# Gathering selected key and value blocks in rows of eight tokens instead of four, in a sparse-attention decoder step

## The chip, the core and the metric

The kernel runs on one core of a Trainium2 chip. Its time is device microseconds of one launch, and the median of three runs counts. The engines are named as in the profile: PE (TensorE, matmuls), PEld (its weight loads), DVE (VectorE), ACT (ScalarE), POOL (GpSimd) and SP (SyncE, which issues most transfers). A gather here is an indirect transfer that POOL issues: each partition gives a row index, and the DMA engines fetch that row from memory into that partition.

## What is computed

Two layers of a decoder run for a prompt of 1024 positions and, with the same weights, for eight samples with one new token each and 4096 past positions in paged caches. Layer 0 has three attention branches and a convolution module; layer 1 is a pooling mixer; each layer ends in a gated feed-forward network. The change touches one branch of layer 0, for the samples alone: the selected blocks.

```python
# nsa_sample, cut
o_c, p_c = compressed_attention(q, t_pos, kcmp, vcmp)      # attention over compressed tokens
idx = select_blocks(p_c, t_pos, ns)                        # 16 blocks of 64 tokens, per sample and group
key_pos = idx[..., None] * SEL_BLOCK + jnp.arange(SEL_BLOCK)
phys = page_table[bi, jnp.clip(key_pos // PAGE_SIZE, 0, n_pages - 1)]
from_pool = pool_s[li, phys, key_pos % PAGE_SIZE, :, gi]   # gather from the paged cache
...
sel = jnp.where((key_pos < past)[..., None, None], from_pool, from_new)
o_s = selected_attention(q, t_pos, idx, sel)               # softmax(q k) v over the gathered tokens
```

Each of the 8 samples has 2 key/value groups, so there are 16 lists of blocks. One block of each list is the one with the new token; the other 15 blocks of 64 tokens with 64 channels come from the cache. That is 15 x 64 x 64 x 4 bytes, or 240 KB, for each list, once for the keys and once for the values.

## The kernel before

All activations lie with channels on partitions and the 1032 columns (1024 prompt positions, then the 8 samples) along the row. The kernel runs an input projection, the compression of the prompt, prompt attention, the output projection, and two feed-forward networks with the pooling mixer between them. Each projection does its matmul in three passes of single-precision parts (`mm3`, `mm3t`). The framework orders each engine's instructions by their place in the program, a priority and its own time model, and places all waits; buffers come from pools with a fixed number of slots (the pool `u` has 16).

The samples' work is a chain of generators. `program` starts it before prompt attention, and `tick`, called after matmuls of the main stream, advances it by a clock of estimated microseconds; its steps run at a lower priority than the main stream and fill gaps in it. The chain goes: `sample_compress` (32 steps; `page_load` brings the pages of the compressed branch, half of them by POOL gathers at L571, half by SP transfers at L569), `dec_window`, `dec_select`, `dec_sel_scores`, `dec_gather_v`, `dec_values`. Prompt attention (`att_s1`, `att_s2`, `pv`) is the main stream at that time, and then `out_proj`.

The steps that the change touches:

- `dec_select` (L829) picks the blocks and turns them into row numbers `vidx`. The rows of the cache are 4 tokens long (256 numbers, 1 KB), so a block has 16 rows. Fifteen blocks are 240 rows, more than the 128 partitions, so there are two halves h: 128 rows (8 blocks) and 112 rows (7 blocks). Two matmuls (L881) spread the block numbers over the partitions.
- `dec_gather_k` (L929) makes a buffer `dw2` and four buffers `ks` of the pool `u`, two samples each, and issues 32 gathers of keys (L939): 16 lists by two halves. Nothing waits between them.
- `dec_sel_scores` (L944) starts 35 units of its clock later. For each sample and half it transposes the keys of four token places with four matmuls (L955), which read every fourth number of the rows, and ACT copies the result back over the rows it came from (the helper L105, output `ks`). Then 16 score matmuls with 512 columns and 16 with 449 (L967), the softmax into `dw2`, and eight transposes of it (L979).
- `dec_gather_v` (L985) starts when `out_proj` has set `self.after` (L1053), and issues 32 gathers of values (L996) into four buffers `vsel` of the pool `u`, which come free as prompt attention ends.
- `dec_values` (L1002) multiplies: 64 matmuls at L1027 read `vsel`.

Of the kernel before, what the change touches and what calls it, by code (L numbers as in the profile page):

```python
# [12 lines left out]
I32 = mybir.dt.int32  # L13
U32 = mybir.dt.uint32
AF = mybir.ActivationFunctionType
ALU = mybir.AluOpType
# [4 lines left out]
P = 128  # L21
D = 1024
TP = 1024
NS = 8
T = TP + NS
# [6 lines left out]
SCALE = 0.125  # L32
KY = 0.8
LAG = 100
DY = 0.6
# [5 lines left out]
class Net:  # L41
# [760 lines left out]
    def dec_prep(self):  # L802
        nc, i = self.nc, self.i
        nd = i["c_dec"].shape[1]
        dw = self.u([P, 2 * T], name="dw")
# [8 lines left out]
        cst = self.cst = dw[:, 0:nd]  # L814
        nc.sync.dma_start(cst, i["c_dec"])
        self.eb, self.own = cst[:64, 16:24], cst[:64, 358:374]
        self.pnt = d(NS, P).rearrange("p (a b) -> p a b", a=2)
# [4 lines left out]
        t = i["page_table"]  # L822
# [6 lines left out]
    def dec_select(self):  # L829
        nc, d, cst, tb = self.nc, self.d, self.cst, self.tb  # L830
        hsum = cst[:64, 0:16]
        esel, iota62, addv = cst[:16, 24:280], cst[:16, 280:342], cst[:, 342:358]
        ps = self.ps(self.to(), [64, 256])
# [44 lines left out]
        nc.vector.tensor_copy(pht, pp)  # L878
        vp = self.ps(self.to(), [P, 2, 16])
        for h in range(2):  # L880
            nc.tensor.matmul(vp[:, h], esel[:, h * P:(h + 1) * P], pht, start=True, stop=True)  # L881
        self.vidx = self.small(P, 32, I32).rearrange("p (a b) -> p a b", a=2)
        nc.vector.scalar_tensor_tensor(self.vidx, vp, 32.0, addv[:, None, :].to_broadcast([P, 2, 16]),
                                       op0=ALU.mult, op1=ALU.add)
        yield DY * 2.0
# [43 lines left out]
    def dec_gather_k(self):  # L929

        nc, i = self.nc, self.i
        self.ksel = []
        self.dw2 = self.u([P, 2 * T], name="dw2")
        for b2 in range(4):
            k = self.u([P, 2, 2, 2, 256], name="ks")
            for n in range(4):
                for h in range(2):
                    m = P - 16 * h
                    nc.gpsimd.indirect_dma_start(out=k[:m, n // 2, h, n % 2], out_offset=None, in_=i["cslc_k"],  # L939
                                                 in_offset=bass.IndirectOffsetOnAxis(  # L940
                                                     ap=self.vidx[:m, h, 4 * b2 + n:4 * b2 + n + 1], axis=0))
            self.ksel.append(k)

    def dec_sel_scores(self):  # L944

        nc = self.nc
        yield WAIT[0]
        for b in range(NS):
            k = self.ksel[b // 2][:, b % 2]
            for h in range(2):  # L950
                m = P - 16 * h
                tp = self.ps(self.to(), [P, 512])
                kt = k[:, h].rearrange("p g c -> p (g c)")
                for e in range(4):
                    nc.tensor.transpose(tp[:, e * m:(e + 1) * m], kt[:m, e:512:4], self.ident[:m, :m])  # L955
                self.acopy(kt[:, :4 * m], tp[:, :4 * m])
                if h:
                    nc.vector.tensor_copy(kt[:, 448:449], self.knew[:, 0, b:b + 1])
                yield DY * 0.4
        dw = self.dw2  # L960
        p = dw[:64, 0:961]
        for h in range(2):
            n = 512 - 63 * h
            ps = self.ps(self.to(), [64, 512])
            for b in range(NS):
                kt = self.ksel[b // 2][:, b % 2, h].rearrange("p g c -> p (g c)")
                nc.tensor.matmul(ps[:, :n], self.qz[:, b], kt[:, :n], start=b == 0, stop=b == NS - 1)  # L967
                yield DY * 0.8
            self.acopy(p[:, 512 * h:512 * h + n], ps[:, :n])
# [4 lines left out]
        self.new_key(p, 960, 0)  # L974
        tp = self.ps(self.to(), [P, 4, 2, 64])
        for h in range(2):
            m = P - 16 * h
            for e in range(4):
                nc.tensor.transpose(tp[:m, e, h], p[:, 512 * h + e * m:512 * h + (e + 1) * m], self.ident[:64, :64])  # L979
        self.pst = dw[:, 1024:1536].rearrange("p (e h b) -> p e h b", e=4, h=2)  # L980
        self.acopy(self.pst[:, :, 0], tp[:, :, 0])
        self.acopy(self.pst[:112, :, 1], tp[:112, :, 1])
        yield WAIT[1]

    def dec_gather_v(self):  # L985
        nc, i = self.nc, self.i
        self.vsel = []
        while not self.after:
            yield DY * 0.4
        for b2 in range(4):  # L990
            v = self.u([P, 4, 2, 256], name="vsel")
            for e in range(4):
                n = 4 * b2 + e
                for h in range(2):
                    m = P - 16 * h
                    nc.gpsimd.indirect_dma_start(out=v[:m, e, h], out_offset=None, in_=i["cslc_v"],  # L996
                                                 in_offset=bass.IndirectOffsetOnAxis(ap=self.vidx[:m, h, n:n + 1],
                                                                                     axis=0))
            self.vsel.append(v)
            yield DY * 0.1  # L1000

    def dec_values(self):  # L1002
# [3 lines left out]
        for hf in range(2):  # L1006
# [15 lines left out]
            for j in (2 * hf, 2 * hf + 1):  # L1022
                o = ov[:, 256 * (j % 2):256 * (j % 2) + 256].rearrange("p (n d) -> p n d", n=4)
                for h in range(2):
                    m = P - 16 * h
                    for e in range(4):
                        nc.tensor.matmul(o, self.pst[:m, e, h], self.vsel[j][:m, :, h, 64 * e:64 * e + 64],  # L1027
                                         start=False, stop=j % 2 == 1 and h == 1 and e == 3)
                        yield DY * 0.45
            nc.vector.tensor_tensor(t[:, 512 * hf:512 * hf + 512].rearrange("p (n d) -> p n d", n=8),  # L1030
# [441 lines left out]
def dec_consts():  # L1472
    c = np.zeros((P, 374), np.float32)
# [5 lines left out]
    for h in range(2):  # L1479
        c[:16, 24 + h * P:24 + (h + 1) * P] = bg[:, None] == (8 * h + p // 16)[None, :]  # L1480
    c[:16, 280:342] = np.arange(62)
    c[:, 342:358] = (bg % 2)[None, :] * 16 + (p % 16)[:, None]
    c[row, 358 + row // 4] = 1.0
    return c


def arrange(a):
# [36 lines left out]
    cs = f["cache_slc_kv"][0].reshape(-1, 64, 2, 2, 64)  # L1524
    r["cslc_k"] = cs[:, :, 0].reshape(-1, 16, 4, 2, 64).transpose(0, 3, 1, 4, 2).reshape(-1, 256)
    r["cslc_v"] = cs[:, :, 1].transpose(0, 2, 1, 3).reshape(-1, 256)
    sw = f["state_win_kv"][0]
# [50 lines left out]
```

## Time and profile before

| | us |
|---|---|
| three runs | 2498.76, 2500.28, 2510.8 |
| median | 2500.28 |
| the profiled execution | 2508.53 |
| its span, first to last instruction | 2506.8 |
| PE busy in it | 2380.4 |
| DVE, ACT, POOL busy | 1324.6, 745.4, 210.2 |

The profile is one execution, taken by the hardware. Times of rows count from the start of its span. An entry such as `L955 PEld LDWEIGHTS ps<-ident,ks` names the line of the kernel, the engine, the operation, and the tiles written and read. A bracket such as `[20.44 <-DVE pt L117]` behind an instruction says how long its engine was idle before it and what ended that wait; "issue" there means that the profile shows nothing that it waited for, and "remote" a release by something that the profile does not show. In stretches (windows), a group `6.49 (x27)` is the busy time of an engine and its instructions, PEclk the granted share of TensorE's full clock (1.00 is 2.4 GHz, 0.50 is 1.2 GHz), then the mean busy share of the 16 DMA engines, and GB/s.

### The profile page before, as it was taken

Reading aid. Unit: us, or ns where it says so; the run is one execution under the profiler, and the core shown is the slowest. Engines: PE = TensorE matmul, PEld = TensorE weight load, DVE = VectorE, ACT = ScalarE, POOL = GpSimd, SP = SyncE. Lnnn points to the kernel's source line nnn. Section 1 sums busy time; section 2 is a strip of 40 time slices with the busy share of each in tenths; the row PEclk is TensorE's granted clock in tenths of the full one; section 3 lists DMA queues with packets and bytes.
Section 4 is the critical chain, followed back from the end, with each engine's and each line's share of the span. In section 5 each row is a group of like instructions: output and inputs, shape, how many; then the busy total and the mean of one; then the engine's idle time right before and its main releaser. Section 6 shows DMA issues by size and latency. Waiting matters only on the chain.

```text
span 2506.8 us, 36521 instructions
## 1 busy us (share of the span) xinstructions
PE 2380.4 (95%) x15040; PEld 2214.4 (88%) x15040; DVE 1324.6 (53%) x2261; ACT 745.4 (30%) x1415; POOL 210.2 (8%) x209
## 2 busy tenths in 40 slices
PE   8999889999876999999999999997999999999998
PEld 7999767677544799999999999986999999999997
DVE  7999565534531463444444444568544444444446
ACT  5113576655541252111111111134311111111102
POOL 0001313243224020000000000000000000000000
PEclk9999899999977999999999999998999999999999
DMA  5131324244116141311111111111211111111101
GB/s 176 35 119 60 120 78 142 84 128 120 40 51 221 59 127 51 118 50 50 52 34 51 51 51 51 42 34 49 71 44 41 51 41 44 51 51 51 51 9 68
DMA packets 79986, 176.77 MB, mean 71 GB/s; under 512 B 15468, under 2 KB 45932, under 8 KB 78316
## 3 DMA queue, kind: packets, MB, share of 16 engines
q1 hardware_dynamic: 70460, 149.68, 19.1%
q0 software_dynamic: 9216, 24.65, 3.3%
q8 instruction: 118, 1.93, 0.3%
q14 instruction: 48, 0.39, 0.0%
q10 hardware_dynamic: 144, 0.11, 0.0%
HBM read 160.51 MB, written 19.01 MB: 72 GB/s over the span
## 4 chain that ended last, share of the span: by engine, by line
PE 88%; DVE 4%; ACT 4%; issue 2%; another core or an unknown queue 1%; DMA 1%; POOL 0%; DVEq 0%; ACTq 0%; POOLq 0%; SPq 0%
PE ps L1114 21%; PE ps L1113 21%; PE ps L1112 21%; PE ps L584 5%; PE ps L743 3%; PE ps L136 3%; PE ps L134 3%; PE ps L135 3%; PE ps L762 2%; PE ps L678 1%; PE ps L679 1%; PE ps L1357 1%; PE ps L967 1%; PE ps L1027 1%
## 5 line engine op out<-in xcount | busy, mean ns | idle before, releaser
L1112 PE MATMUL ps<-hh,w 128*128 128x344 f32 x2112 | 678.5, 321 | 14.6 <-DVE sg L1209 13.9
L1113 PE MATMUL ps<-hl,w 128*128 128x344 f32 x2112 | 678.5, 321 | 0.2 <-DVE hl L1371 0.2
L1114 PE MATMUL ps<-hh,w 128*128 128x344 f32 x2112 | 678.4, 321 | 0.0
L1227 DVE TENSOR_TENSOR x<-x,ps 128x344 f32<-128x344 f32 x528 | 267.0, 512 | 288.1 <-PE ps L1114 286.2
L1112 PEld LDWEIGHTS ps<-hh,w 128*128 128x128 f32 x2112 | 398.9, 189 | 16.9 <-DVE sg L1209 14.8
L1113 PEld LDWEIGHTS ps<-hl,w 128*128 128x128 f32 x2112 | 398.8, 189 | 1.0 <-DVE hl L1371 0.4
L1114 PEld LDWEIGHTS ps<-hh,w 128*128 128x128 f32 x2112 | 398.7, 189 | 0.5
L105 ACT ACTIVATE w<-raw 128x1024 fp32r<-128x1024 f32 x170 | 177.7, 1057 | 708.0 <-PE ps L1114 674.8
L1112 PE MATMUL ps<-ah,w 128*128 128x344 f32 x1056 | 338.9, 321 | 0.7 <-ACT rt L1125 0.7
L1114 PE MATMUL ps<-ah,w 128*128 128x344 f32 x1056 | 338.4, 320 | 0.0
L1113 PE MATMUL ps<-al,w 128*128 128x344 f32 x1056 | 337.8, 320 | 0.0
L1209 DVE TENSOR_TENSOR sg<-ps,rs 128x688 f32<-128x688 f32 x132 | 115.2, 873 | 310.2 <-PE ps L1114 309.6
L109 DVE TENSOR_TENSOR w<-raw,w 128x1024 fp32r<-128x1024 f32 x170 | 211.2, 1243 | 90.9 <-ACT w L105 88.9
L1112 PEld LDWEIGHTS ps<-ah,w 128*128 128x128 f32 x1056 | 198.7, 188 | 1.5 <-ACT rt L1125 0.9
L1113 PEld LDWEIGHTS ps<-al,w 128*128 128x128 f32 x1056 | 198.4, 188 | 0.5
L1114 PEld LDWEIGHTS ps<-ah,w 128*128 128x128 f32 x1056 | 198.4, 188 | 0.0
L1210 ACT ACTIVATE sg<-sg 128x344 f32<-128x344 f32 x132 | 64.9, 492 | 376.6 <-DVE sg L1209 376.5
L571 POOL DMA_INDIRECT pg<-ccmp,aux x128 | 126.5, 989 | 471.4 <-PE ps L136 241.4
L134 PE MATMUL ps<-hh,w 128*128 128x344 f32 x456 | 150.2, 330 | 11.8 <-ACT w L105 9.9
L136 PE MATMUL ps<-hh,w 128*128 128x344 f32 x456 | 149.3, 329 | 4.9 <-DVE w L109 4.9
L135 PE MATMUL ps<-hl,w 128*128 128x344 f32 x456 | 148.7, 326 | 0.3 <-DVE hl L109 0.3
L392 DVE SCALAR_TENSOR_TENSOR y<-ext,vec,y 128x1011 f32<-128x1011 f32 (+28 forms) x120 | 147.5, 1271 | 0.5
(304 smaller groups left out, 2965.4 us busy)
## 6 DMA issues: line engine op xcount, KB each, us to landing
raw<-w_gate SPq DMA_DIRECT2D x44, 512.0 KB
raw<-w_up SPq DMA_DIRECT2D x44, 512.0 KB
raw<-w_down SPq DMA_DIRECT2D x44, 512.0 KB
pg<-ccmp SPq DMA_DIRECT2D x128, 128.0 KB
raw<-w_in SPq DMA_DIRECT2D x22, 512.0 KB
raw<-w_out SPq DMA_DIRECT2D x16, 512.0 KB
x<-xt SPq DMA_DIRECT2D x12, 344.0 KB
x<-xt SPq DMA_DIRECT2D x4, 1032.0 KB
```

What stands on the lines that cost most here:

```text
L105: return self.nc.scalar.activation(out, in_, AF.Copy, scale=scale)
L109: (eng or self.nc.vector).tensor_tensor(lo, src, hi.bitcast(F32), op=ALU.subtract)
L134: nc.tensor.matmul(ps, wh, xh[k], start=first and k == 0, stop=False)
L135: nc.tensor.matmul(ps, wh, xl[k], start=False, stop=False)
L136: nc.tensor.matmul(ps, wl, xh[k], start=False, stop=last and k == n - 1)
L392: nc.vector.scalar_tensor_tensor(y[:, z:TP], e[:, 0:TP - z], self.cw[:, j, k:k + 1], y[:, z:TP], op0=ALU.mult, op1=ALU.add)
L571: nc.gpsimd.indirect_dma_start(out=dst, out_offset=None, in_=i["ccmp"], in_offset=bass.IndirectOffsetOnAxis(ap=self.pidx[:, m:m + 1], axis=0))
L584: nc.tensor.matmul(ps[:, s], self.w1[:, s, k * P:(k + 1) * P], raw[:, :, s, k].rearrange("p a (g c) -> p g a c", g=2), start=k == 0, stop= ...
L1112: nc.tensor.matmul(ps, wh, xh[k], start=n == 0, stop=False)
L1113: nc.tensor.matmul(ps, wh, xl[k], start=False, stop=False)
L1114: nc.tensor.matmul(ps, wl, xh[k], start=False, stop=n == len(order) - 1)
L1227: nc.vector.tensor_tensor(xs, xs, ps, op=ALU.add)
```

## The change

The cache rows become 8 tokens long (512 numbers, 2 KB). A block then has 8 rows and 15 blocks have 120 (`NSEL`), so that one gather of 120 partitions fetches a whole list. The 32 gathers of keys become 16, and the 32 of values become 16; the bytes stay the same, and so does the number of transposes (64), of score matmuls (32, now with 480 and 481 columns) and of value matmuls (64, now all with 120 rows). The transposes read every eighth number. One matmul spreads the block numbers, and its table shrinks the constants from 374 to 246 columns.

The transposed keys of a sample need 961 columns in one piece, so they no longer go back over the same rows. A new buffer `kx` takes those of samples 0 and 1, and sample b from 2 on writes over the rows of sample b-2, which have been transposed by then. `dw2` is no buffer of its own any more: it lies over the rows of samples 6 and 7, which nobody needs once they are transposed. The number of buffers of the pool `u` is the same. The waits by the samples' clock (`yield`) stay.

```diff
+NSEL = 120
...
-        vp = self.ps(self.to(), [P, 2, 16])
-        for h in range(2):
-            nc.tensor.matmul(vp[:, h], esel[:, h * P:(h + 1) * P], pht, start=True, stop=True)
-        self.vidx = self.small(P, 32, I32).rearrange("p (a b) -> p a b", a=2)
-        nc.vector.scalar_tensor_tensor(self.vidx, vp, 32.0, addv[:, None, :].to_broadcast([P, 2, 16]),
-                                       op0=ALU.mult, op1=ALU.add)
+        vp = self.ps(self.to(), [P, 16])
+        nc.tensor.matmul(vp, esel, pht, start=True, stop=True)
+        self.vidx = self.small(P, 16, I32)
+        nc.vector.scalar_tensor_tensor(self.vidx, vp, 16.0, addv, op0=ALU.mult, op1=ALU.add)
...
         self.ksel = []
-        self.dw2 = self.u([P, 2 * T], name="dw2")
+        self.kx = self.u([P, 2, 1024], name="kx")
         for b2 in range(4):
-            k = self.u([P, 2, 2, 2, 256], name="ks")
+            k = self.u([P, 2, 1024], name="ks")
             for n in range(4):
-                for h in range(2):
-                    m = P - 16 * h
-                    nc.gpsimd.indirect_dma_start(out=k[:m, n // 2, h, n % 2], out_offset=None, in_=i["cslc_k"],
-                                                 in_offset=bass.IndirectOffsetOnAxis(
-                                                     ap=self.vidx[:m, h, 4 * b2 + n:4 * b2 + n + 1], axis=0))
+                nc.gpsimd.indirect_dma_start(out=k[:NSEL, n // 2, 512 * (n % 2):512 * (n % 2) + 512], out_offset=None, in_=i["cslc_k"],
+                                             in_offset=bass.IndirectOffsetOnAxis(
+                                                 ap=self.vidx[:NSEL, 4 * b2 + n:4 * b2 + n + 1], axis=0))
             self.ksel.append(k)
...
+        kts = [t[:, s] for t in [self.kx] + self.ksel[:3] for s in range(2)]
         for b in range(NS):
             k = self.ksel[b // 2][:, b % 2]
             for h in range(2):
-                m = P - 16 * h
-                tp = self.ps(self.to(), [P, 512])
-                kt = k[:, h].rearrange("p g c -> p (g c)")
+                tp = self.ps(self.to(), [P, 4 * NSEL])
                 for e in range(4):
-                    nc.tensor.transpose(tp[:, e * m:(e + 1) * m], kt[:m, e:512:4], self.ident[:m, :m])
-                self.acopy(kt[:, :4 * m], tp[:, :4 * m])
+                    nc.tensor.transpose(tp[:, e * NSEL:(e + 1) * NSEL], k[:NSEL, 4 * h + e:1024:8],
+                                        self.ident[:NSEL, :NSEL])
+                self.acopy(kts[b][:, 4 * NSEL * h:4 * NSEL * (h + 1)], tp)
...
-        dw = self.dw2
-        p = dw[:64, 0:961]
+        dw = self.dw2 = self.ksel[3].rearrange("p s c -> p (s c)")
+        p = dw[:64, 0:8 * NSEL + 1]
...
         for b2 in range(4):
-            v = self.u([P, 4, 2, 256], name="vsel")
+            v = self.u([P, 4, 512], name="vsel")
             for e in range(4):
                 n = 4 * b2 + e
-                for h in range(2):
-                    m = P - 16 * h
-                    nc.gpsimd.indirect_dma_start(out=v[:m, e, h], out_offset=None, in_=i["cslc_v"],
-                                                 in_offset=bass.IndirectOffsetOnAxis(ap=self.vidx[:m, h, n:n + 1],
-                                                                                     axis=0))
+                nc.gpsimd.indirect_dma_start(out=v[:NSEL, e], out_offset=None, in_=i["cslc_v"],
+                                             in_offset=bass.IndirectOffsetOnAxis(ap=self.vidx[:NSEL, n:n + 1],
+                                                                                 axis=0))
...
-    r["cslc_k"] = cs[:, :, 0].reshape(-1, 16, 4, 2, 64).transpose(0, 3, 1, 4, 2).reshape(-1, 256)
-    r["cslc_v"] = cs[:, :, 1].transpose(0, 2, 1, 3).reshape(-1, 256)
+    r["cslc_k"] = cs[:, :, 0].reshape(-1, 8, 8, 2, 64).transpose(0, 3, 1, 4, 2).reshape(-1, 512)
+    r["cslc_v"] = cs[:, :, 1].transpose(0, 2, 1, 3).reshape(-1, 512)
```

## Rows read from the trace of the kernel before

**Rows 1.** The page: busy times of the engines, and three lines of the 40 slices of the span (62.7 us each).
```profile
PE 2380.4 (95%) x15040; PEld 2214.4 (88%) x15040; DVE 1324.6 (53%) x2261; ACT 745.4 (30%) x1415; POOL 210.2 (8%) x209
PE   8999889999876999999999999997999999999998
PEclk9999899999977999999999999998999999999999
DMA  5131324244116141311111111111211111111101
```

**Rows 2.** Who PE waited for, the whole span: total us, times, longest.
```profile
PE ps L703 <- DVE pt L117: 20.4, 1, 20.4
PE ps L1112 <- DVE sg L1209: 13.9, 4, 6.2
...
PE ps L1113 <- issue: 5.8, 3, 2.3
```

**Rows 3.** Windows: the stretch, its length, busy time of PE, PEld, DVE, ACT and POOL, PEclk, DMA share, GB/s. First a run of page gathers, then the two runs of gathers that the change touches.
```profile
503.00:545.00 42.00, 39.53 (x332) 33.81 (x331) 14.09 (x39) 17.30 (x55) 26.18 (x28) 1.00 0.56 165
665.00:705.00 40.00, 13.37 (x80) 7.77 (x79) 6.71 (x10) 8.62 (x16) 30.52 (x32) 0.69 0.34 98
757.00:793.00 36.00, 23.27 (x69) 11.45 (x70) 5.52 (x8) 5.14 (x9) 27.14 (x29) 0.78 0.91 309
```

**Rows 4.** Windows over the two stretches in which PE stands still, and what follows the first.
```profile
676.60:711.00 34.40, 6.49 (x27) 3.79 (x27) 1.30 (x3) 3.78 (x6) 21.67 (x23) 0.56 0.29 86
778.90:799.00 20.10, 4.27 (x12) 3.14 (x12) 1.00 (x5) 1.85 (x3) 11.23 (x13) 0.60 0.69 238
712.00:718.00 6.00, 6.00 (x25) 3.96 (x25) 2.63 (x10) 3.33 (x9) 0.00 (x0) 0.50 0.01 3
708.00:712.00 4.00, 2.66 (x12) 1.48 (x10) 1.60 (x3) 1.73 (x9) 0.00 (x0) 0.50 0.00 0
800.00:804.00 4.00, 4.00 (x16) 3.51 (x16) 0.73 (x2) 0.21 (x1) 0.00 (x0) 0.57 0.30 88
```

**Rows 5.** The timeline across engines around the gathers of keys: start, duration, instruction, idle time before it.
```profile
665.04 0.94 POOL L939 DMA_INDIRECT ks<-cslc_k,sm  x1 [65.78 <-DVE sm L883]
676.43 0.22 PE L683 MATMUL ps<-mb 128*128 128x128 bf16 x1
682.12 0.60 ACT L105 ACTIVATE pt<-ps 128x512 f32<-128x512 f32 x1 [7.74 <-remote]
696.14 0.60 ACT L105 ACTIVATE ks<-ps 128x512 f32<-128x512 f32 x1 [11.57 <-remote]
704.10 0.93 POOL L939 DMA_INDIRECT ks<-cslc_k,sm  x1 [0.30 <-issue]
704.57 0.69 DVE L117 COPY pt<-ps 128x512 f32<-128x512 f32 x1 [28.46 <-remote]
705.32 0.37 PE L703 MATMUL ps<-mb 128*128 128x256 bf16 x1 [20.44 <-DVE pt L117]
709.46 0.34 PE L955 MATMUL ps<-ident,ks 112*128 112x112 f32 x1 [0.58 <-issue]
710.16 0.35 PE L955 MATMUL ps<-ident,ks 112*128 112x112 f32 x1 [0.36 <-issue]
710.26 0.59 ACT L105 ACTIVATE pt<-ps 56x512 f32<-56x512 f32 x1 [13.52 <-remote]
```

**Rows 6.** The timeline around the gathers of values.
```profile
757.21 9.67 PE L967 MATMUL ps<-ks,sm 128*64 128x512 f32 x16 [0.63 <-ACT ks L105]
757.32 1.27 POOL L996 DMA_INDIRECT vsel<-cslc_v,sm  x1 [5.55 <-ACT ks L105]
767.56 6.24 PE L967 MATMUL ps<-ks,sm 128*64 128x449 f32 x16 [0.68 <-issue]
788.50 0.70 SPq L1083 DMA_DIRECT2D x<-xt  x1
788.53 0.45 PE L1113 MATMUL ps<-zl,w 128*128 128x344 f32 x1 [2.35 <-issue]
792.87 0.92 POOL L996 DMA_INDIRECT vsel<-cslc_v,sm  x1 [0.30 <-issue]
796.23 0.45 PE L1113 MATMUL ps<-zl,w 128*128 128x344 f32 x1 [1.65 <-issue]
797.63 0.45 PE L1114 MATMUL ps<-zh,w 128*128 128x344 f32 x1 [0.95 <-issue]
798.57 0.49 PE L1113 MATMUL ps<-zl,w 128*128 128x344 f32 x1
```

**Rows 7.** The timeline of POOL in the run of page gathers: the first and last of one group of four, and the first of the next.
```profile
509.68 0.94 POOL L571 DMA_INDIRECT pg<-ccmp,aux  x1 [1.56 <-DMA pg<-ccmp,aux]
513.43 0.95 POOL L571 DMA_INDIRECT pg<-ccmp,aux  x1 [0.30 <-issue]
515.88 0.94 POOL L571 DMA_INDIRECT pg<-ccmp,aux  x1 [1.51 <-PE ps L743]
```

**Rows 8.** POOL's gathers, from what is listed for their lines and tiles: minimum, median and maximum in ns, first and last start in us.
```profile
L571 POOL DMA_INDIRECT pg<-ccmp,aux x128: 940/946/2944, 231.7 to 598.3; - x128
L939 POOL DMA_INDIRECT ks<-cslc_k,sm x32: 924/938/1345, 665.0 to 704.1; - x32
L996 POOL DMA_INDIRECT vsel<-cslc_v,sm x32: 918/943/1272, 733.0 to 792.9; - x32
```

**Rows 9.** The DMA queue that POOL's gathers use: packets, MB, share of 16 engines.
```profile
q0 software_dynamic: 9216, 24.65, 3.3%
```

**Rows 10.** Groups of instructions by shape, 660 to 870 us: busy us, mean ns. Transposes of the keys, and for comparison a weight load of neighbouring numbers.
```profile
L955 PEld LDWEIGHTS ps<-ident,ks 128*128 128x128 f32 x32 | 4.9, 211 | 2.1 <-issue 1.2 <-ACT ks L105 0.9
L679 PEld LDWEIGHTS ps<-kd,q 128*128 128x128 f32 x24 | 4.9, 202 | 0.2
L967 PE MATMUL ps<-ks,sm 128*64 128x512 f32 x16 | 9.7, 774 | 0.6 <-ACT ks L105 0.6
```

More of the change, by code (lines that the diff above doesn't have):

```diff
@@ L815, in dec_prep @@
         nc.sync.dma_start(cst, i["c_dec"])
-        self.eb, self.own = cst[:64, 16:24], cst[:64, 358:374]
+        self.eb, self.own = cst[:64, 16:24], cst[:64, 230:246]
         self.pnt = d(NS, P).rearrange("p (a b) -> p a b", a=2)
@@ L831, in dec_select @@
         hsum = cst[:64, 0:16]
-        esel, iota62, addv = cst[:16, 24:280], cst[:16, 280:342], cst[:, 342:358]
+        esel, iota62, addv = cst[:16, 24:152], cst[:16, 152:214], cst[:, 214:230]
         ps = self.ps(self.to(), [64, 256])
@@ L950, in dec_sel_scores @@
             for h in range(2):
-                m = P - 16 * h
-                tp = self.ps(self.to(), [P, 512])
-                kt = k[:, h].rearrange("p g c -> p (g c)")
+                tp = self.ps(self.to(), [P, 4 * NSEL])
                 for e in range(4):
-                    nc.tensor.transpose(tp[:, e * m:(e + 1) * m], kt[:m, e:512:4], self.ident[:m, :m])
-                self.acopy(kt[:, :4 * m], tp[:, :4 * m])
+                    nc.tensor.transpose(tp[:, e * NSEL:(e + 1) * NSEL], k[:NSEL, 4 * h + e:1024:8],
+                                        self.ident[:NSEL, :NSEL])
+                self.acopy(kts[b][:, 4 * NSEL * h:4 * NSEL * (h + 1)], tp)
                 if h:
-                    nc.vector.tensor_copy(kt[:, 448:449], self.knew[:, 0, b:b + 1])
+                    nc.vector.tensor_copy(kts[b][:, 8 * NSEL:8 * NSEL + 1], self.knew[:, 0, b:b + 1])
                 yield DY * 0.4
-        dw = self.dw2
-        p = dw[:64, 0:961]
+        dw = self.dw2 = self.ksel[3].rearrange("p s c -> p (s c)")
+        p = dw[:64, 0:8 * NSEL + 1]
         for h in range(2):
-            n = 512 - 63 * h
             ps = self.ps(self.to(), [64, 512])
+            n = 4 * NSEL + h
             for b in range(NS):
-                kt = self.ksel[b // 2][:, b % 2, h].rearrange("p g c -> p (g c)")
-                nc.tensor.matmul(ps[:, :n], self.qz[:, b], kt[:, :n], start=b == 0, stop=b == NS - 1)
+                nc.tensor.matmul(ps[:, :n], self.qz[:, b], kts[b][:, 4 * NSEL * h:4 * NSEL * h + n],
+                                 start=b == 0, stop=b == NS - 1)
                 yield DY * 0.8
-            self.acopy(p[:, 512 * h:512 * h + n], ps[:, :n])
+            self.acopy(p[:, 4 * NSEL * h:4 * NSEL * h + n], ps[:, :n])
         r = self.softmax64(p, p)
@@ L973, in dec_sel_scores @@
         yield DY * 2.0
-        self.new_key(p, 960, 0)
-        tp = self.ps(self.to(), [P, 4, 2, 64])
-        for h in range(2):
-            m = P - 16 * h
[L978 to L982, printed above, removed]
+        self.new_key(p, 8 * NSEL, 0)
+        tp = self.ps(self.to(), [P, 8, 64])
+        for e in range(8):
+            nc.tensor.transpose(tp[:NSEL, e], p[:, e * NSEL:(e + 1) * NSEL], self.ident[:64, :64])
+        self.pst = dw[:, 1024:1536].rearrange("p (e b) -> p e b", e=8)
+        self.acopy(self.pst[:NSEL], tp[:NSEL])
         yield WAIT[1]
@@ L990, in dec_gather_v @@
         for b2 in range(4):
-            v = self.u([P, 4, 2, 256], name="vsel")
+            v = self.u([P, 4, 512], name="vsel")
             for e in range(4):
                 n = 4 * b2 + e
-                for h in range(2):
-                    m = P - 16 * h
-                    nc.gpsimd.indirect_dma_start(out=v[:m, e, h], out_offset=None, in_=i["cslc_v"],
-                                                 in_offset=bass.IndirectOffsetOnAxis(ap=self.vidx[:m, h, n:n + 1],
-                                                                                     axis=0))
+                nc.gpsimd.indirect_dma_start(out=v[:NSEL, e], out_offset=None, in_=i["cslc_v"],
+                                             in_offset=bass.IndirectOffsetOnAxis(ap=self.vidx[:NSEL, n:n + 1],
+                                                                                 axis=0))
             self.vsel.append(v)
@@ L1023, in dec_values @@
                 o = ov[:, 256 * (j % 2):256 * (j % 2) + 256].rearrange("p (n d) -> p n d", n=4)
[L1024 to L1029, printed above, removed]
+                for e in range(8):
+                    nc.tensor.matmul(o, self.pst[:NSEL, e], self.vsel[j][:NSEL, :, 64 * e:64 * e + 64],
+                                     start=False, stop=j % 2 == 1 and e == 7)
+                    yield DY * 0.45
             nc.vector.tensor_tensor(t[:, 512 * hf:512 * hf + 512].rearrange("p (n d) -> p n d", n=8),
@@ L1472, in dec_consts @@
 def dec_consts():
-    c = np.zeros((P, 374), np.float32)
+    c = np.zeros((P, 246), np.float32)
     p = np.arange(P)
@@ L1478, in dec_consts @@
     bg = np.arange(16)
[L1479 to L1483, printed above, removed]
+    c[:16, 24:152] = bg[:, None] == (p // 8)[None, :]
+    c[:16, 152:214] = np.arange(62)
+    c[:, 214:230] = (bg % 2)[None, :] * 8 + (p % 8)[:, None]
+    c[row, 230 + row // 4] = 1.0
     return c
```

## The prediction

> **What bounds the kernel now.** Read the page first: PE is busy 95% of the span, and its line of slices has one dent, slices 11 to 13 (690 to 815 us), where PEclk falls to 7 tenths [rows 1]. Then read who PE waited for. Over 2507 us almost nothing adds up, and the longest single wait, 20.4 us, ends with a DVE copy of prompt attention, an operation that this change does not touch [rows 2]. So the question is what held DVE. Windows around the dent show two stretches in which PE hardly works: 676.6 to 711 us, with 6.5 us of PE work in 34.4, and 778.9 to 799, with 4.3 in 20.1 [rows 4]. Each lies in a run of POOL gathers: 32 for keys from 665.0 to 704.1, 29 for values from 757.3 to 792.9 [rows 5, 6]. PE, ACT and DVE stop together there. Three of the waits end with "remote", and the timeline has operands that were ready long before [rows 5]. Where PE does run, its instructions come on a grid of 0.70 us: two transposes at 709.46 and 710.16, matmuls at 788.53, 796.23, 797.63, each a multiple of 0.7 apart; one transfer issue on SP takes 0.70 us at that time [rows 5, 6]. After the last gather the grid lasts some 5 to 6 us and then ends at once (710.3 and 798.5).
>
> Is it bandwidth? No: in the keys' run the DMA engines are 34% busy at 98 GB/s, and at 708 to 712 us they move nothing while the grid still holds [rows 3, 4]. Is it gathers as such? The page gathers at 503 to 545 us move more (165 GB/s) and PE works 39.5 of 42 us beside them [rows 3]. The difference that I see is the rate: page gathers come four at a time, then a pause, 6.20 us from group to group, 1.55 us for each [rows 7]; the keys' come every 39.06 / 31 = 1.26 us [rows 5]. So I read it as a queue behind the gathers that all engines' instructions share, and that serves a gather in between 1.26 and 1.55 us. If the 32 gathers of keys are what it works off from 665.0 to 710.3, it needs 45.2 / 32 = **1.41 us for each gather**, twice 0.70. At 1.26 us a backlog grows slowly, and PE feels it only 11.6 us after the first gather (676.6).
>
> What the two stretches cost: PE stands still 34.4 - 6.5 = 27.9 us and 20.1 - 4.3 = 15.8 us [rows 4]. Its clock is granted at 0.5 (1.2 GHz) after it has stood still, to about 718 and 803.4 us [rows 4]; some 11.4 us and 7.7 us of busy time then lie at half speed, which costs 5.7 and 3.9 us. Together 33.6 us for keys and 19.7 us for values, 53 us in all. As PE is the bound before and after, what comes back here comes off the end.
>
> **The change part by part.** *Gathers of keys.* 16 instead of 32, of 120 rows each. Gathers with 128 and with 112 rows take nearly the same on POOL (924 to 1345 ns, median 938 [rows 8]), so I keep 1.26 us for each. The last starts at 665.0 + 15 x 1.26 = 683.9 us, and at 1.41 us each the queue is empty at 665.0 + 16 x 1.41 = 687.6, say 688 us. The backlog grows at the same rate as before, so PE still stops at 676.6. It stands still some 11.4 us, of which it works about 1.5; then the clock is low again for some 7 us of work and a little before, which I price at 4.5 us. Cost then: 9.9 + 4.5 = 14.4 us instead of 33.6. Gain 19 us.
>
> *Gathers of values.* Before, 29 of 32 came in one run, and PE stopped 778.9 - 757.3 = 21.6 us after its start, later than for keys, because until 773.8 PE ran the long score matmuls, few instructions for the queue to carry [rows 6]. Now about 14 are left in the run; they need 14 x 1.41 = 19.7 us, which ends before PE would stop. The whole 19.7 us should go. Bounds: 0 (the stall stays) and 19.7. I take 19.
>
> *What is late next.* With PE not stopped, it reaches the output projection's next tiles earlier, while the DMA engines are 91% busy from 757 to 793 us [rows 3]: values, weights, x and window values all come there. The bytes stay, but a gather moves twice as many in the same 1.26 us, so other transfers get less while it runs. Until 773.8 PE has the score matmuls to do [rows 6]; they are the cover. Without it PE would wait for z or x. Bound: 0 to 8 us (36 us at 0.91 leave 3 us free; one 1 MB load of x at 309 GB/s is 3.4 us). I take 1.
>
> *Transposes.* 64 as before. Every fourth number costs a weight load 211 ns, neighbouring numbers 202 [rows 10]: 9 ns for a step of 16 bytes. A step of 32 bytes does not occur in the trace; between nothing and a doubled load, 64 x 0.211 = 13.5 us. The nearest row says little, so I take 64 x 9 ns = 0.6 us. The copies by ACT move 480 columns instead of 512 or 448, and the score matmuls 961 columns in all as before: nothing. Half the matmul records of the row numbers and one ACT copy fall away: under 0.5 us, on gaps.
>
> *New waits.* The copy of sample b waits for the transposes of sample b-2. They stand before it in PE's order and their copies before it in ACT's, and a sample takes several us; no cost. `dw2` over the last rows waits for the last transposes, which the score matmuls have already waited for; no cost. `kx` takes the place of `dw2` among the 16 buffers, and the last key buffer now lives to the end as `dw2` did, so the value buffers come free as before. The first transposes need two gathers as before; PE's order may shift a little because the framework's time model sees shorter gathers; I have no row for that, and take ±4 us.
>
> Sum: 19 + 19 - 1 - 0.6 = 36.4, and the profiled execution of 2508.5 us would become 2472. The execution is 0.33% above the median of 2500.3, so against the median: 2500.3 - 36.4 = **2464 us**.
>
> **The rivals.** *(a) The queue counts bytes, and the kernel gets slower.* Then a gather of 2 KB rows needs 2 x 1.41 = 2.82 us. PE stopped when the backlog was about 1.5 us of work (9.3 gathers at 1.41 - 1.26 each); that is now reached after 1 or 2 us, at 667, while 16 x 2.82 = 45 us still end at 711. For keys the stop is 8 to 11 us longer. For values it begins at some 760 us and ends at 798; the score matmuls, two instructions each, fall onto the grid: 38 us / 2.8 us a pair are 13 pairs, worth 6.5 us, so some 31 us are lost instead of 19.7. Together about 22 us: 2522. It decides from where a gather takes over 2.2 us: there 16 gathers stop PE as long as before (from 667 to 701). For it: twice the bytes at the same pace is new. Against: page gathers at 165 GB/s stop nothing, and in the values' run, at 309 GB/s, PE stopped later than in the keys' run at 98 [rows 3, 4].
>
> *(b) It counts packets; no change.* The queue's 9216 packets are 48 for each of the 192 gathers [rows 8, 9], 3 for each of 16 DMA engines. If one of three carries no rows, 8 rows of 1 KB go in 2 packets, and 2 KB rows need 4 + 1: 80 packets, 1.67 times as many, 2.35 us for each gather. Keys then cost 3 us more, values between 19 less and 6 more: 2485 to 2509, most likely near 2500. The Trainium skill (DMA: Bandwidth & Descriptors, section SWDGE vs HWDGE vs iDMA) says that a software-issued packet is preferably at most 4096 bytes; the 48 packets agree, and by that rule, if packets are what is served, the change would bring nothing. A gather that costs POOL twice as much for longer rows gives the same time: the run is as long as before.
>
> *(c) Both stops vanish.* If the queue needs a long run and 20 us are not enough, all 53 us come back: 2447. Against: PE stopped after 11.6 us before.
>
> **How the numbers follow.** Forecast (a stop of 11 us for keys, none for values): 0.55, between 2455 and 2480 by the bounds above. (c) 0.12. (b) 0.18. (a) 0.15. Range for 8 in 10: 2444 (case c with the shift of order) to 2508 (all of b; of a only its edge). A measurement of this kernel can tell about 0.5%, 12.5 us, from no change. Faster by more than that: forecast and (c), and the part of (b) in which values gain, 0.70; slower, (a) without its mild part, 0.13; the rest, 0.17.
>
> **What would show it.** Right: 16 gathers of keys some 1.26 us apart, PE busy again about 688 us, no grid of 0.7 us in the values' run and PEclk 1.00 after it. Wrong: gathers of keys 2 us or more apart; PE stopped from about 667 us on (bytes or packets); a weight load at the new transposes far over 211 ns; PE idle after the score matmuls with DMA named as what it waited for. If the stops move elsewhere without a run of gathers, my reading of the cause is wrong.

## The result and the profile after

| | us |
|---|---|
| before, four runs | 2499.57 (2498.76 to 2510.80) |
| after, four runs | 2463.53 (2454.91 to 2467.96) |
| after / before | 0.9837, 95% interval 0.9815 to 0.9859 |
| the profiled execution after | 2467.96, its span 2466.2 |

By the medians 36.0 us came off; 36.4 were forecast (2464). PE's idle time in the two profiled spans fell from 2506.8 - 2380.4 = 126.4 us [rows 1] to 2466.2 - 2374.1 = 92.1.

The page of the kernel after: busy times of the engines, two lines of slices (61.7 us each), and POOL's DMA queue (packets, MB, share of 16 engines).

```profile
PE 2374.1 (96%) x15038; PEld 2212.8 (90%) x15038; DVE 1323.6 (54%) x2261; ACT 745.5 (30%) x1414; POOL 185.6 (8%) x177
...
PE   8999899999989999999999999988999999999998
...
PEclk9999899999989999999999999989999999999999
...
q0 software_dynamic: 8704, 24.65, 3.5%
```

PEclk had 7 and 7 where the dent lies, in the twelfth and thirteenth slice [rows 1]; now 8 and 9 stand there. POOL's queue carries the same 24.65 MB in 8704 packets: 128 page gathers with 48 and 32 new ones with 80.

The timeline of the kernel after around the gathers of keys (start, duration, instruction, idle time before it):

```profile
668.03 0.99 POOL L936 DMA_INDIRECT ks<-cslc_k,sm  x1 [65.80 <-DVE sm L883]
...
679.35 0.57 ACT L106 ACTIVATE kx<-ps 128x480 f32<-128x480 f32 x1 [4.28 <-remote]
...
687.33 0.98 POOL L936 DMA_INDIRECT ks<-cslc_k,sm  x1 [0.30 <-issue]
...
689.26 0.69 DVE L118 COPY pt<-ps 128x512 f32<-128x512 f32 x1 [9.52 <-remote]
690.01 0.37 PE L704 MATMUL ps<-mb 128*128 128x256 bf16 x1 [6.44 <-DVE pt L118]
690.80 0.57 ACT L106 ACTIVATE kx<-ps 128x480 f32<-128x480 f32 x1 [7.53 <-remote]
```

Sixteen gathers, (687.33 - 668.03) / 15 = 1.29 us apart. The last wait with "remote" ends at 690.8, and (690.8 - 668.0) / 16 = 1.42 us for each gather: the 1.41 of the kernel before, at twice the bytes. The wait of 20.44 us for the DVE copy [rows 2, 5] is now 6.44.

Windows of the kernel after (stretch, length, busy PE, PEld, DVE, ACT, POOL, PEclk, DMA share, GB/s): before the stop, in it, behind it, and the values' run.

```profile
660.00:676.00 16.00, 16.00 (x108) 10.28 (x106) 11.06 (x29) 10.29 (x23) 6.14 (x7) 1.00 0.30 85
676.00:690.00 14.00, 5.65 (x30) 2.92 (x27) 2.42 (x6) 3.02 (x4) 9.56 (x10) 0.64 0.68 187
690.00:703.00 13.00, 12.99 (x63) 8.93 (x63) 5.97 (x14) 6.70 (x20) 0.00 (x0) 0.60 0.02 9
...
736.00:776.00 40.00, 36.05 (x158) 24.91 (x157) 11.60 (x17) 9.86 (x14) 13.16 (x12) 0.91 1.00 305
```

A stop beside the keys remains, 14 - 5.65 = 8.4 us, with a clock of 0.60 behind it. Beside the values there is no grid and no wait with "remote"; PE lacks 4 us there while the DMA engines are full (share 1.00). What it waits for is a transfer:

```profile
PE ps L1102 <- ACT zh L106: 3.0, 1, 3.0
```

(PE's waits after, whole span: total us, times, longest. `zh` is a part of `z`, loaded for the output projection.) The new transposes, by shape, 680 to 800 us: busy us and mean ns.

```profile
L951 PEld LDWEIGHTS ps<-ident,ks 120*128 120x128 f32 x60 | 8.6, 201 | 5.5 <-issue 3.9 <-ACT ks L106 0.6 <-ACT pt L106 0.4
```

A step of 32 bytes takes 201 ns, not more than the 211 of a step of 16 [rows 10].

### The profile page after: what moved, and what is told of

Its sections match the earlier page's. It is cut to its first block, busy times and chain, and to the rows that moved or that the text cites. A ratio compares the mean times of both kernels' runs of the same rounds, so it can differ in the third digit from the quotient of the medians.

```text
span 2466.2 us, 36458 instructions
## 1 busy us (share of the span) xinstructions
PE 2374.1 (96%) x15038; PEld 2212.8 (90%) x15038; DVE 1323.6 (54%) x2261; ACT 745.5 (30%) x1414; POOL 185.6 (8%) x177
## 3 DMA queue, kind: packets, MB, share of 16 engines
q0 software_dynamic: 8704, 24.65, 3.5%
## 4 chain that ended last, share of the span: by engine, by line
PE 66%; DVE 2%; ACT 0%; DMA 0%; issue 0%; POOL 0%; DVEq 0%; POOLq 0%; ACTq 0%
PE ps L1102 21%; PE ps L1104 21%; PE ps L1103 21%; PE ps L1347 1%; PE ps L1017 1%; PE ps L1120 0%; DVE z L1327 0%; PE ps L1012 0%; PE ps L963 0%; DVE zs L1303 0%; DVE hs L1303 0%; DVE x L1395 0%; DVE x L1349 0%; DVE hl L1361 0%; DVE x L1217 0%; DVE zs L1260 0%
```

## The experiments

Two theories stood at the start. **Pace:** gathers with row numbers that follow each other in under 1.42 us fill something that all engines share, each counts the same, and the stop begins when enough of them are left unserved (the backlog). **Rivals:** the amount counts (rows, packets or bytes), or the new order of PE's work did it, or POOL being busy. These runs were made on three chips: e1 to e4 on one, e5 to e8 on a second, e9 to e12 on a third, each time beside runs of the kernel before on the same chip (medians 2499.94, 2501.69 and 2440.51 us). Which chip the first measurement was made on is not on record; its kernel before took 2499.57 us, as on the first two. The kernel after itself was run again on the third chip alone (e11). The last of the three medians is a result of its own, below. A ratio is to the kernel before on the same chip, with its 95% interval.

### e1: the gathers of keys split again

```diff
-                nc.gpsimd.indirect_dma_start(out=k[:NSEL, ...], ... self.vidx[:NSEL, ...])
+                for a, z, vidx in ((0, 64, self.vidx), (64, NSEL, self.vidx2)):
+                    nc.gpsimd.indirect_dma_start(out=k[a:z, ...], ... vidx[:z - a, ...])
```

(`vidx2` holds the row numbers of the upper 56 rows.) Rows, bytes and layout stay; the number of gathers doubles.

> The changed kernel, but each gather of keys is split into two, of 64 and 56 rows of 2 KB: 32 gathers of keys again, with the rows and bytes of the changed kernel, and 16 of values. Count theory (the shared queue serves each gather in about 1.41 us, whatever it carries): the stop beside the keys' run returns in full, from about 12 us after its first gather to about 710 us, 19 us more than the changed kernel, about 2482 us. Rows theory (it serves rows, 11 ns each): a gather of 64 rows needs 0.7 us, the run never outpaces the queue, no stop at all, about 2448 us. Order theory (the gain came from another order of instructions and the shared buffers, not from the gathers): as the changed kernel, about 2463 us.

Measured: 2489.95 us, 0.9959 of before (0.9941 to 0.9977), 26 us above the kernel after by the medians and 30 by the ratios; the count theory gave 19. Timeline of e1:

```profile
662.34 0.91 POOL L941 DMA_INDIRECT ks<-cslc_k,sm  x1 [65.78 <-DVE sm L883]
...
700.54 0.92 POOL L941 DMA_INDIRECT ks<-cslc_k,sm  x1 [0.30 <-issue]
...
707.29 0.69 DVE L118 COPY pt<-ps 128x512 f32<-128x512 f32 x1 [33.48 <-remote]
```

Windows of e1, the same columns as above:

```profile
662.30:676.00 13.70, 10.45 (x69) 6.38 (x67) 6.40 (x12) 5.75 (x12) 10.40 (x11) 1.00 0.37 105
676.00:692.00 16.00, 0.00 (x0) 0.00 (x0) 0.00 (x0) 0.00 (x0) 11.94 (x14) 0.55 0.33 98
692.00:708.00 16.00, 2.10 (x8) 0.90 (x9) 0.69 (x1) 3.03 (x4) 7.32 (x8) 0.50 0.22 66
```

Half the rows, and each gather still takes its (708.0 - 662.3) / 32 = 1.43 us. For 16 us PE, DVE and ACT do nothing at all. The bytes of each gather are those of the kernel before, 128 KB or less, and the 240 KB of the kernel after took no longer. So the count of gathers decides here, at this pace; rows, bytes and order fall. The gathers come a little faster than before's, every 38.20 / 31 = 1.23 us, which fits the longer stop; no run tests that.

### e2: the gathers of values split again

The same edit at the gathers of values.

> The changed kernel, but each gather of values is split into two, of 64 and 56 rows: 16 gathers of keys, 32 of values. Count theory: a stop beside the values' run returns, 15 to 20 us, about 2480 us, and the keys' stop stays as in the changed kernel. Rows theory and order theory: about 2463 us.

Measured: 2474.87 us, 0.9908 (0.9878 to 0.9939), 11 us above the kernel after by the medians and 18 by the ratios. A window, and the timeline in it:

```profile
748.00:764.00 16.00, 5.67 (x15) 4.12 (x15) 1.89 (x4) 2.40 (x3) 7.57 (x9) 0.52 0.36 97
```
```profile
751.33 0.45 PE L1108 MATMUL ps<-zl,w 128*128 128x344 f32 x1 [1.66 <-issue]
753.45 0.45 PE L1109 MATMUL ps<-zh,w 128*128 128x344 f32 x1 [1.67 <-issue]
...
762.00 0.56 ACT L106 ACTIVATE ks<-ps 64x480 f32<-64x480 f32 x1 [11.35 <-remote]
```

The grid is back: matmuls 2.1 us apart, three times 0.70, and an ACT copy released by "remote". So the halved number of value gathers is what took it away. What that was worth, 11 us or the 19 of the prediction, these few runs can't tell apart: they scatter over 13 us, and so do those of the kernel after.

### e3: the kernel after, its gathers paced

```diff
+    def pause(self, out, n):            # a POOL multiplication into the buffer that the gather fills next
+        v = self.vidx[:, 0:1].bitcast(F32).to_broadcast([P, n])
+        self.nc.gpsimd.tensor_tensor(out[:, 0:n], v, v, op=ALU.mult)
...
+            self.pause(k[:, 0], 512)    # ahead of the four gathers of a key buffer
...
+                if e % 2 == 0:
+                    self.pause(v[:, e], 344)
```

> The changed kernel with a pause between gathers: POOL multiplies 512 numbers before each four gathers of keys, and 344 before each two of values, into places that the gathers then overwrite. POOL needs 1.6 to 1.8 us for each gather of keys, more than the 1.41 us of the queue. Count theory: no stop beside the keys' run, the 14 to 16 us that the changed kernel still loses there come back, about 2448 us. If it is the sheer number of gathers and not their pace: as the changed kernel, 2463 us, or some us more. If a busy POOL is what stops the others, whatever it does: the stop grows with the longer run, about 2470 us.

Measured: 2461.71 us, 0.9854 (0.9826 to 0.9882): no different from the kernel after (0.9837). Windows of e3:

```profile
676.00:692.00 16.00, 14.96 (x98) 9.32 (x98) 10.38 (x20) 10.16 (x21) 7.41 (x9) 1.00 0.47 132
...
700.00:740.00 40.00, 35.12 (x224) 30.48 (x223) 15.95 (x22) 15.53 (x24) 19.01 (x17) 0.96 0.90 257
740.00:780.00 40.00, 31.83 (x128) 21.95 (x127) 7.32 (x12) 7.69 (x12) 0.00 (x0) 0.87 0.42 147
```

The framework did not spread the pauses evenly: the first nine gathers come in threes, with a pause ahead of each three, and the last seven in one row. Over the whole run they are 22.46 / 15 = 1.50 us apart, less than the 1.6 to 1.8 expected but more than 1.42. The keys' stop is gone, the clock is 1.00 there, and yet the time is the same. From 700 to 780 us PE stands still 80 - 66.95 = 13.1 us, and its clock is 0.96 and 0.87; in the kernel after it stands still 4.6 us, at 0.99 and 0.91:

```profile
700.00:740.00 40.00, 39.37 (x265) 26.64 (x264) 24.04 (x37) 27.62 (x47) 7.50 (x7) 0.99 0.36 112
740.00:780.00 40.00, 36.05 (x156) 24.62 (x156) 10.15 (x17) 8.95 (x13) 10.01 (x10) 0.91 0.97 297
```

PE arrives earlier at the output projection and waits there. Its waits in e3 from 700 to 780 us begin with these:

```profile
PE ps L1109 <- DVE x L1077: 4.6, 1, 4.6
...
PE ps L1109 <- ACT zh L106: 2.3, 1, 2.3
```

DVE itself was released there by the transfer of `x`, and `zh` is made from the transfer of `z`. Between the two stand 2.9 us for an ACT copy of keys, behind ACT's wait of 7.95 us for `z`. No wait of PE in this stretch names POOL or the values. e5 and e6 ask how much of this is due to the values' transfers.

### e4: the kernel before, its gathers paced

The same `pause` in the kernel before: 512 numbers for every four gathers of keys, 256 for every two of values. All 64 gathers stay.

> The kernel before, rows of four tokens and 64 gathers, with the same pause: POOL multiplies 512 numbers before each four gathers of keys and 256 before each two of values. Count theory with pace: both stops go although the number of gathers stays, 40 to 53 us less than before, 2447 to 2460 us. If the number of gathers decides: as before, 2500 us. If a busy POOL decides: slower than before, 2510 us.

Measured: 2471.94 us, 0.9887 (0.9861 to 0.9913): 28 us less with nothing but a slower POOL. Windows of e4, the last of them in the values' run:

```profile
660.00:676.00 16.00, 15.78 (x111) 9.87 (x110) 11.04 (x22) 11.34 (x28) 13.47 (x15) 1.00 0.25 74
676.00:688.00 12.00, 11.53 (x71) 6.67 (x70) 5.83 (x9) 6.39 (x13) 9.43 (x10) 1.00 0.33 96
688.00:711.00 23.00, 12.16 (x58) 6.87 (x55) 6.54 (x12) 7.93 (x14) 15.73 (x17) 0.68 0.28 82
...
740.00:780.00 40.00, 38.69 (x154) 21.95 (x152) 12.76 (x19) 9.93 (x17) 32.46 (x35) 0.95 0.87 297
```

The framework spaced the pauses of the keys evenly only at first, one for two gathers; from 673 us on, six and eight gathers follow each other 1.26 us apart, and from 688 on PE stops. Inside one kernel the pace switches the stop on. Beside the values all 32 gathers of 1 KB rows are still there, from 731.49 to 778.91 us or 47.42 / 31 = 1.53 us apart on average, and PE works 38.7 of 40 us; of the stop, waits of 1.3 and 1.8 us at the run's end are left (ACT and DVE, "remote", at 781.69). That POOL is busy is not it: it works 13.5 of 16 us ahead of the stop, and 15.7 of 23 in it.

### e5 and e6: after and paced after, without the gathers of values

```diff
-                nc.gpsimd.indirect_dma_start(out=v[:NSEL, e], ...)
+            nc.vector.memset(v, 0.0)
```

> The changed kernel without its 16 gathers of values (DVE sets the buffers to zero, so the output of the samples is wrong in that part). It asks what the values' transfers still cost beside the output projection. In the changed kernel PE waited 3.0 and 0.9 us there for z, with the DMA engines full. Transfers theory: these waits go, about 4 us, and the keys' stop of 8.4 us and its cold clock stay: 2458. Rival (the waits at the output projection are the order of the instructions, not the transfers): no change, 2463.

> The paced changed kernel (e3) without its 16 gathers of values (zeros instead, output of the samples wrong in that part). It asks where the 14 us went that the paced kernel did not show although the keys' stop was gone. Transfers theory: PE came earlier to the output projection and waited there for transfers; without the values' bytes these waits are gone, and the time falls by the keys' 14 to 16 us below the kernel without values that isn't paced: 2458 - 14 = 2444. Rival (the keys' stop itself was cheap, because a part of the work done after it was brought forward): within 4 us of the kernel without values that isn't paced, 2455 to 2460.

Measured: e5 2468.44 us (0.9866, 0.9848 to 0.9884), e6 2455.42 us (0.9819, 0.9803 to 0.9836). Windows of e5, then of e6:

```profile
676.00:688.00 12.00, 5.08 (x25) 3.14 (x25) 1.48 (x4) 3.27 (x5) 6.88 (x7) 0.60 0.57 170
...
700.00:740.00 40.00, 35.87 (x211) 20.83 (x210) 27.65 (x36) 27.40 (x45) 0.00 (x0) 0.91 0.44 142
740.00:780.00 40.00, 40.00 (x182) 26.41 (x181) 9.91 (x15) 6.71 (x10) 0.00 (x0) 1.00 0.47 168
```
```profile
676.00:688.00 12.00, 11.78 (x79) 7.20 (x78) 8.58 (x18) 7.19 (x19) 9.05 (x10) 1.00 0.60 176
...
700.00:740.00 40.00, 35.15 (x187) 24.56 (x186) 22.41 (x27) 20.04 (x32) 0.00 (x0) 0.91 0.57 188
740.00:780.00 40.00, 40.00 (x192) 27.63 (x191) 7.15 (x12) 6.98 (x12) 0.00 (x0) 1.00 0.44 158
```

Two answers. With the values left out, pacing the keys is worth 13.0 us, near the 14.4 that the prediction gave the stop left beside them: in e3 this gain is given back around the output projection, where PE now stands still 4.9 us (e6) instead of 13.1 (e3). e6 also leaves out the pauses among the values, so it doesn't separate the values' bytes from those pauses; that e3's waits name transfers and never POOL speaks for the bytes. But leaving the values out of the unpaced kernel brings nothing (e5 against after): there PE still loses 4.1 us from 700 to 780, with z, weights and x alone. My expectation for e5 missed; the values cost time in the paced kernel alone. Both kernels are also some 10 us slower than I gave them, and I have no row for that.

### e7 and e8: the kernel before with plain transfers of keys

```diff
-                    nc.gpsimd.indirect_dma_start(out=k[:m, n // 2, h, n % 2], ..., in_=i["cslc_k"], in_offset=...)
+                    nc.gpsimd.dma_start(k[:m, n // 2, h, n % 2], i["cslc_k"][r:r + m])     # e8: nc.sync
```

> The kernel before, its 32 gathers of keys replaced by 32 plain transfers of the same shapes, issued by POOL, of fixed rows (output of the samples wrong in that part); small DVE copies of the row numbers hold them back until the row numbers are there. The gathers of values stay. Theory: the queue is loaded by the gathers with row numbers; plain transfers come without the stop beside keys: 2500 - 33 = 2467. Rival: every transfer that POOL issues loads it, whatever it reads: the stop stays, about 2500, with the grid of 0.70 us.

> As the kernel with plain transfers from POOL, but SP issues the 32 transfers of keys (fixed rows, output of the samples wrong in that part). Theory: no stop beside the keys, since nothing of POOL's queue is used: 2467, plus some us because SP issues the weights' and pages' loads later, 2467 to 2480. Rival (many small transfers at once stop the engines, whoever issues them): about 2500.

Measured: e7 2467.89 us (0.9869, 0.9852 to 0.9885), e8 2470.15 us (0.9873, 0.9849 to 0.9896). Windows of e7 beside its transfers of keys and beside its gathers of values, and the line of POOL's issues:

```profile
662.00:680.00 18.00, 18.00 (x128) 12.06 (x127) 11.20 (x24) 13.36 (x33) 17.42 (x32) 1.00 0.72 219
740.00:762.00 22.00, 5.39 (x13) 3.05 (x12) 1.39 (x4) 0.00 (x0) 12.28 (x14) 0.59 0.62 202
```
```profile
L941 POOL DMA_DIRECT2D ks<-cslc_k x32 | 17.6, 574 | 66.0 <-DVE ks L936 66.0
```
```profile
q0 software_dynamic: 9216, 24.65, 3.2%
```

POOL issues 32 transfers in 17.6 us, one per 0.55, into the same queue, with the packets and bytes of the kernel before, and PE works 18.00 of 18 us. Sixty us later the run of the values' gathers is under way and PE has 5.4 of 22. So it is the transfers with row numbers, and neither POOL's queue nor its packets as such. (The plain transfers also read neighbouring rows; whether the row numbers or the scattered rows matter, no run separates.) With SP as the issuer, e8, the result is the same. And 2501.69 - 2467.89 = 33.8 us is about what the keys' stop cost; the prediction read 33.6 from the windows.

### e9 to e12: a third chip

e9 paces the keys alone, one pause of 256 numbers ahead of every two gathers, the order on POOL fixed; e12 adds a later start of the values (`yield 16.0` ahead of them); e11 is the kernel after itself. e10 is the kernel before with such pauses everywhere. Every second pause among the keys writes over the rows that the gather just ahead of it has brought, so those rows are lost, and it waits for that gather to land: keys come 63.48 / 31 = 2.05 us apart, all 64 gathers 1.9.

> The changed kernel with a POOL instruction of about 0.55 us ahead of every two gathers of keys (their order is fixed), so that a gather comes every 1.5 us; the gathers of values are not paced. The keys' stop goes (14 us at most). Theory from the last runs: most of it is given back at the output projection, where PE now arrives while the DMA engines are full: 2452 to 2462, 1 to 11 us below the changed kernel. Rival (the second pauses, those among the values, were what cost the paced kernel its gain): 2449.

> The kernel before with its 64 gathers of 1 KB rows, a POOL instruction of about 0.55 us ahead of every two of them, and their order on POOL fixed, so that nowhere more than two come at 1.26 us. If the pace alone decides, both stops go with all 64 gathers in place, and the time is at most that of the changed kernel: 2455 to 2465. If the number of gathers in a run decides, a stop stays beside keys and beside values: 2480 to 2500.

> The changed kernel once more, beside the paced ones on the same chip: 2463.5 as before, 8.4 us of stop beside the keys.

> As the kernel with paced keys, and the gathers of values start 16 units of the samples' clock later, past the point where PE waited for z and x at the output projection. If the values' bytes take these loads' share, PE waits less there: 3 to 8 us below the kernel with paced keys alone, 2450. If z, x and the weights fill the DMA engines by themselves, no change, or PE waits for the values later: 2456 to 2464.

| on this chip | us | / before |
|---|---|---|
| before | 2440.51 | |
| e9, keys paced | 2439.04 | 0.9997 (0.9988 to 1.0005) |
| e11, after | 2441.98 | 1.0010 (1.0001 to 1.0018) |
| e12, keys paced, values late | 2448.92 | 1.0034 (1.0021 to 1.0047) |
| e10, before, all paced | 2463.15 | 1.0093 (1.0078 to 1.0107) |

None of the four expected times fits: the kernel before takes 60 us less here than on the other two chips, and the change is worth nothing. Timeline and windows of e11, which is the kernel after, instruction for instruction:

```profile
651.96 0.99 POOL L936 DMA_INDIRECT ks<-cslc_k,sm  x1 [65.83 <-DVE sm L883]
...
671.58 0.98 POOL L936 DMA_INDIRECT ks<-cslc_k,sm  x1 [0.30 <-issue]
```
```profile
652.00:673.00 21.00, 21.00 (x151) 13.89 (x150) 13.33 (x28) 15.60 (x37) 15.98 (x16) 1.00 0.64 179
...
700.00:740.00 40.00, 32.11 (x142) 19.95 (x141) 11.45 (x14) 11.32 (x18) 15.68 (x14) 0.96 0.94 267
```

The gathers come at the same 1.3 us and last the same 0.98 us, and PE works 21.00 of 21 us beside them. Not one wait from 230 to 800 us ends with "remote". What is left is the output projection, where PE loses 7.9 us with the DMA engines at 0.94. So e9 has no stop to take away, and e10 can't say whether the pace alone decides: it shows that keys 2.05 us apart come too late there (PE waits 10.5 us in all for the transfers into `ks`). For e12 PE waits longer for `zh`, 5.5 us in all; the later values didn't clear the way for z.

## Why the prediction was right, and where it was not

- **The reading** (two stops made by the pace of the gathers, one gather per 1.41 us) holds wherever the kernel before takes 2500 us: 1.42 us with 120 rows, 1.43 with 64 and 56 (e1), no stop when paced (e3, e4's values, and e4's keys while their pauses last). e7 narrows it to transfers with row numbers. What it is that all engines share, no run shows.
- **Keys:** forecast 14.4 us left, measured 8.4 us of stop and 13.6 us of work at half clock, which costs 6.8: 15.2 us, or 13.0 by e6 against e5. Before, read in the same way, it was 27.9 + 6.8 = 34.7, so 19.5 us came back; 19 were forecast. The first wait with "remote" ends 11 us after the first gather, at 679.35, and the last at 690.8 instead of 688, since the run began 3 us later.
- **Values:** the grid went, as forecast. *What is late next* was the mis-sized term: 1 us taken, bound 8. PE loses 4.0 us from 736 to 776, and does 5.8 us of work at half clock, 2.9 us more: 6.9. So 13 us came back of 19.9, not 18. The cause given for it (a gather of 2 KB rows leaves other transfers less) is not borne out: e5 has no gathers of values and loses 4.1 us all the same.
- **The sum** came out in part by luck. The two profiled executions are 2508.53 - 2467.96 = 40.6 us apart; 36.4 were forecast for them. Keys and values make 32.5 of it. Some 7 us more came from waits that the prediction did not count: outside the two stops PE stood still another 4.8 us from 660 to 820 us before, and 0.7 after, and it did 6.2 us of work at half clock at 756 to 762, ahead of the values' stop, which cost 3.1. The windows (before, then after; the stretches behind the first of each are those of half clock) give 48.6 - 13.0 = 35.6 us less idle time and (27.95 - 19.41) / 2 = 4.3 us less by the clock, 39.9 in all:

```profile
660.00:820.00 160.00, 111.43 (x547) 67.31 (x546) 47.12 (x85) 53.45 (x100) 61.31 (x64) 0.80 0.40 128
680.54:718.09 37.55, 13.53 (x54) 8.49 (x54) 4.93 (x13) 8.11 (x20) 18.69 (x20) 0.50 0.23 69
755.63:762.46 6.83, 6.20 (x11) 2.11 (x12) 2.51 (x4) 0.54 (x1) 4.04 (x4) 0.50 0.98 339
782.94:803.42 20.48, 8.22 (x25) 6.86 (x26) 2.14 (x4) 0.21 (x1) 8.41 (x9) 0.50 0.54 178
```
```profile
660.00:780.00 120.00, 107.05 (x593) 71.46 (x592) 52.00 (x101) 55.51 (x104) 33.21 (x32) 0.89 0.57 170
680.02:700.50 20.48, 13.61 (x57) 8.84 (x58) 5.01 (x13) 8.08 (x20) 6.46 (x7) 0.50 0.35 98
744.88:751.70 6.82, 5.80 (x12) 3.15 (x13) 0.88 (x1) 1.24 (x2) 2.42 (x2) 0.50 1.06 266
```

- **Transposes:** 0.6 us taken; 201 ns against 211, nothing.
- **Rivals.** (a) Bytes: no; twice the bytes, the same 1.42 us. (b) Packets: its count was right, 80 for each new gather. The Trainium skill's rule that a packet is preferably at most 4096 bytes (DMA: Bandwidth & Descriptors, section SWDGE vs HWDGE vs iDMA) agrees with both counts, if one packet more for each of the 16 engines is taken to carry no rows, as the prediction assumed. But the time does not follow packets: gathers of 48 and of 80 are served in the same time, and e7's plain transfers, 48 packets each, make no stop. (c) Not both stops vanished.
- **What the prediction did not hold open:** that the stop depends on the machine and not on the program alone. Its forecast holds where the stop is; on the third chip it would have been 36 us wrong. That the kernel before has no stop on that chip is argued from its time and from e11's trace; no trace of before was taken there. What makes the chips differ, the chip itself or what else was at work on it, stays open.

"Page gathers stop nothing" was too strong as well. Windows were read at 503 to 545 us alone. Last page gather of the kernel after, then of e11:

```profile
601.29 0.95 POOL L572 DMA_INDIRECT pg<-ccmp,aux  x1 [0.30 <-issue]
```
```profile
585.19 0.95 POOL L572 DMA_INDIRECT pg<-ccmp,aux  x1 [0.30 <-issue]
```

The same program starts them at the same 231.3 us in both executions and is 16 us earlier at the last on the third chip. Groups of four at 1.25 us cost something too where the stop exists: four waits end with "remote" in this part of the kernel after, 8.3 us in all, the longest ones 3.24 us and, at 322.11 us, 3.19; e11 has none. How much of the 16 us is due to the gathers, no run shows. The kernel before has such waits as well, so they are in no term of the sum.

## What to carry to other kernels

When several engines stop together beside a run of gathers, on waits that end with "remote" and with the DMA engines not full (0.22 to 0.69 busy here), count the gathers and not the bytes. Fewer and longer gathers, plain transfers where the rows are known, or a short POOL instruction between gathers are then worth a try. Before such an edit is credited, measure both kernels on more than one chip: this one was worth 36 us in the first measurement and nothing on the chip of e9 to e12. And what comes back before a stretch that is full of transfers may be given back there (e3: the keys' stop of some 13 us gone, 8.5 us more standing still some 30 us later, and a lower clock).

## What the runs showed of the hardware

- On two of the three chips of the experiments, transfers with row numbers that POOL issues 1.23 to 1.29 us apart stop PE, ACT and DVE or slow them to a grid of 0.70 us, beginning 8 to 12 us into a run of keys and lasting 3 to 7 us past the last. The time served for each, worked out from the first gather to the end of the stop, is 1.41 to 1.43 us for 56 to 128 rows, of 1 KB or 2 KB. Runs that average 1.50 us (e3, keys) and 1.53 (e4, values) make no stop, or one of 2 us; nothing between 1.29 and 1.50 was run.
- Plain transfers from POOL, 0.55 us apart, do nothing of the kind (e7).
- On the third chip sixteen gathers 1.3 us apart make no stop (e11).
- A gather costs POOL 0.98 us for 120 rows of 2 KB, 0.91 for 64 of them and 0.94 for 128 of 1 KB [rows 8], and 0.30 us to the next: of 2 KB rows, 64 instead of 120 save 0.07 us.
